# A hybrid encoder trunk: the two gated heads of a pair end together, and their farthest level is computed as keys times values, then queries

## The chip, the core and the metric

The kernel runs on one core of one Trainium2 chip. The metric is device microseconds of one execution. The engines that matter here are TensorE (PE: matmuls and transposes), VectorE (DVE), ScalarE (ACT: activations, copies out of PSUM, and DMA issues on its own queue), and SyncE (SP), whose queue loads most weights. Each engine works through its own instructions strictly in the order in which the program stands for it, and semaphores make it wait for the others.

## The reference, cut to what matters

Two layers work on 512 tokens of width 1024, in float32. Each is a half-step feed-forward block, a mixer, and a second half-step block. The mixer is where the change lies:

```python
proj = rmsnorm(x, mix_norm) @ w_in          # na_q, na_k, na_v, g_q, g_k, g_v, g_r, gate codes
na_o  = rmsnorm(merge_heads(neighbourhood_attention(na_q, na_k, na_v, na_rpb)), na_gain)   # 8 heads of 64
log_g = log_sigmoid(code @ w_gate + b_gate) / 16          # one for each direction
o_fwd = gla_chunked(qg, kg, vg, log_gf, True)             # 4 gated heads, keys 64 wide, values 128 wide
o_bwd = flip(gla_chunked(flip(qg), flip(kg), flip(vg), flip(log_gb), False))
gla_o = merge_heads(rmsnorm(o_fwd + o_bwd, gla_gain)) * silu(g_r)
x = x + concatenate([na_o, gla_o]) @ w_out
```

Gated linear attention is a sum over earlier (forward) and later (backward) tokens of `(q_t . decayed k_s) v_s`. The kernel computes it as a hierarchy of levels: a token pair whose distance first shows at block size h is handled at level h, where keys and queries carry the decay up to the border between two neighbouring blocks of h tokens. The farthest level, h = 256, joins the two halves of the sequence.

## The kernel before, in words

Activations lie transposed: 128 channels on partitions, 512 tokens along the free axis. A float32 product with a weight tile is made of three fp32r matmuls: `split` cuts an operand into a rounded high part (ACT) and the remainder (DVE), and `mm3` multiplies high by high, high by low, low by high. Products between activations use plain float32.

**Streams.** `mixer` runs four generators through `interleave`: `gla_all(0)` (gated heads 0 and 1), `na_all` (neighbourhood attention), `gla_all(1)` (gated heads 2 and 3), and `fillers`, the projections that remain, then the output projection. A stream yields either a key that must be in `got`, or a pair of planned times. In each round every stream that is ready takes its steps, then waiting transposes (`turns`) are made, then the filler gets about `SLOT` = 5.3 planned microseconds. This sets the program's order. For TensorE that order is kept (`pinned`). The other engines' instructions are put in an order of their own by the scheduler of the build, so the code doesn't tell it; the built program does.

**Fillers.** `PAIRS` is the order of the projection tiles. `v..` are neighbourhood values, `gv..` gated values, `gr..` the gates that pass through silu. A gated value tile is transposed (`turn`) before use. After the last tile, `op_part(c, 0, 4)` multiplies the neighbourhood half by `w_out` for the eight output tiles c; then come, for c below 4, heads 0 and 1 (`op_part(c, 4, 2)`), and behind the mixer, in the stage that the profile calls OP, heads 2 and 3 (`op_part(c, 6, 2)`) and all four gated heads for the c above.

**Gated heads.** `gla_levels(pr)` builds, for both heads of pair pr, the matrices `at` (levels up to 64), `am` (level 128) and `af` (level 256, four tiles of 128x512). `gla_out` sums values times these in PSUM, takes the root mean square over the head's 128 channels, scales, and multiplies by silu of the gate.

**The row of a root mean square.** `rsqrt_ms` is used for the neighbourhood row and for every gated head: the squares are split (`sqh` on ACT, `sql` on DVE), two matmuls with ones sum them into the bank `bank`, and `rsqrt_row` evaluates it:

```python
MM(ps, onr, h, start=True, stop=False)
MM(ps, onr, l, start=False, stop=True)
...
S.activation(r, ps, AF.Ln, bias=epsc, scale=1.0 / n)
S.activation(r, r, AF.Exp, scale=-0.5)
S.activation(t, ps, AF.Identity, bias=epsc, scale=1.0 / n)
```

In the profile these are `M_r<-M_tp` (Ln), `M_ms<-M_tp` (Identity) and `M_r<-M_r` (Exp), followed by three DVE operations.

**PSUM.** It has eight banks of 128x512: four named `mm`, two `sc`, and one each of `tp` and `o`. Every transpose goes through the one `tp` bank and has to wait until ACT has copied the one before out of it; `rsqrt_ms` uses `tp`, or `sc` for the second head of a pair.

**SBUF pools.** `TAGS` gives the number of 128x512 buffers for each tag; `g0` and `g1` hold everything of pair 0 and of pair 1.

Of the kernel before, what the change touches and what calls it, by code (L numbers as in the profile page):

```python
# [26 lines left out]
FAL = 1.4  # L27
HEAD = 9
MMB = 4
GOT = ('mm', 'mm')  # L30
WARM = 13
NAP = 4.0
SLOT = 5.3
# [10 lines left out]
         ('gk1', 'gq1'),  # L44
         ('q3', 'k3'),
         ('v2', 'v3'),
         ('gr0', 'gr1'),
         ('gv2', 'gv3'),
         ('gv0', 'gv1'),
         ('gr2', 'gr3'))  # L50
COLS = {"q": 0, "k": 512, "v": 1024, "gq": 1536, "gk": 1792, "gv": 2048, "gr": 2560}
TAGS = {'sl': 12, 'g0': 8, 'g1': 8, 'na': 6, 'ws': 5}
NPR = 12
NDF = 3
OPT = 2.56
# [5 lines left out]
def trunk_kernel(ctx, tc, xin, wgu, wdn, win, wcode, wgate, wout, vec, rpbt,  # L61
# [39 lines left out]
    def sl(name="s", dt=F32, tag="sl"):  # L101
        return sp.tile([P, T], dt, tag=tag, name=nm(name), bufs=TAGS[tag])
# [11 lines left out]
    def psum(tag):  # L114
        pool = {"mm": pm, "sc": ps2}.get(tag, ps1)
        return pool.tile([P, T], F32, tag=tag, name=nm(tag))
# [7 lines left out]
    def MM(*args, **kw):  # L124
        return pinned(PE.matmul(*args, **kw))  # L125

    def TR(*args):
        return pinned(PE.transpose(*args))  # L128
# [48 lines left out]
    def paired(mms):  # L177

        for ps, lhs, rhs, kw in mms:
            MM(ps, lhs, rhs, **kw)  # L180
# [396 lines left out]
    def seq_out(a):  # L577
        return a.rearrange("p (r u c) -> p u r c", r=8, u=8)

    def unit_in(a):  # L580
        return a.rearrange("p (u r c) -> p u r c", u=8, r=8)

    def mixer(l):
# [25 lines left out]
        gla = [{}, {}]  # L609

        def gla_gates(pr):
            g = gla[pr]
            for d in range(2):
                gs, pk = sl("gs", F32, f"g{pr}"), sl("pk", F32, f"g{pr}")
                pg = psum("sc" if pr == 0 else ("o", "tp")[d])
                cs = slice(d * 256 + pr * P, d * 256 + (pr + 1) * P)
                MM(pg, wgh[:, cs], cr, start=True, stop=False)
                MM(pg, wgl[:64, cs], cr[:64], start=False, stop=True)
                b = lvec(l, 5 + 2 * d + pr)
                ab, mn = sl("ab", F32, "ws"), sl("mn", F32, "ws")  # L620
                S.activation(ab, pg, AF.Abs, bias=b)
                V.tensor_scalar(mn, pg, b, 0.0, ALU.add, ALU.min)
                S.activation(ab, ab, AF.Exp, scale=-1.0)
                S.activation(ab, ab, AF.Ln, bias=1.0)
                V.tensor_tensor(gs, mn, ab, op=ALU.subtract)
                prev = gs
                for h in (2, 4, 8, 16, 32, 64, 128):
                    n = T // h
                    cur = pk[:, GOFF[h]:GOFF[h] + n]
                    pv = prev.rearrange("p (b two) -> p two b", two=2)  # L630
                    V.tensor_tensor(cur, pv[:, 0, :], pv[:, 1, :], op=ALU.add)
                    prev = cur
                S.activation(gs, gs, AF.Exp, scale=1.0 / 16.0)
                S.activation(pk[:, :508], pk[:, :508], AF.Exp, scale=1.0 / 16.0)
                g["t1", d], g["tp", d] = gs, pk
# [11 lines left out]

        def gla_levels(pr):
            g = gla[pr]
            gla_gates(pr)  # L650
            yield 1.8, 6.0
            yield ("gq", pr)
            qa, ka = got["gq", pr], got["gk", pr]
# [41 lines left out]
            for li, h in enumerate((1, 2, 4, 8, 16, 32, 64, 128)):  # L695
# [45 lines left out]
                elif h2 == 128:  # L741
                    pss = psum("sc"), psum("sc")
                    mms = []
                    for s in range(4):
                        t = s ^ 1
                        kk, qq = (KF, QF) if s < t else (KB, QB)
                        mms += [(pss[hh][:, s * P:(s + 1) * P], kk[rows[hh], s * P:(s + 1) * P],
                                 qq[rows[hh], t * P:(t + 1) * P], SS) for hh in (1, 0)]
                    paired(mms)
                    for hh in range(2):  # L750
                        g["m", hh] = sl("am", F32, f"g{pr}")
                        S.activation(g["m", hh], pss[hh], AF.Copy)
                    done = 1.0
                else:
                    for half in range(2):
                        pss = psum("sc"), psum("sc")
                        kk, qq = (KF, QF) if half == 0 else (KB, QB)
                        o = 256 * (1 - half)
                        paired([(pss[hh][:, j * 256:(j + 1) * 256],
                                 kk[rows[hh], (2 * half + j) * P:(2 * half + j + 1) * P], qq[rows[hh], o:o + 256], SS)  # L760
                                for j in range(2) for hh in (1, 0)])
                        for hh in range(2):
                            g["f", hh, half] = sl("af", F32, f"g{pr}")
                            S.activation(g["f", hh, half], pss[hh], AF.Copy)
                        yield 1.0, FAL

        def post_gv(h0):
            def post(i, o, r):
# [25 lines left out]
        def osplit(src, k, gain):  # L794
            ohl[k] = pair("oh", gain, src)

        def gla_out(hd, tag):
            g = gla[hd // 2]
            hh = hd % 2
            yield ("gs", hd)  # L800
            yield ("gv", hd)
            po = psum(tag)
            v = got["gv", hd]

            def vs(s):
                return v[:, s * P:(s + 1) * P]

            for t in range(4):
                dst = po[:, t * P:(t + 1) * P]
                half = 1 - t // 2  # L810
                fa = g["f", hh, half]
                s1 = t ^ 1
                MM(dst, vs(t), g["at"][hh][:, t * P:(t + 1) * P], start=True, stop=False)
                MM(dst, vs(s1), g["m", hh][:, s1 * P:(s1 + 1) * P], start=False, stop=False)
                for j in range(2):
                    o = j * 256 + (t % 2) * P
                    MM(dst, vs(2 * half + j), fa[:, o:o + P], start=False, stop=(j == 1))
            tag = GOTT[hd // 2]
            on, sq = sl("on", F32, tag), sl("sq", F32, tag)
            S.activation(sq, po, AF.Square)  # L820
            S.activation(on, po, AF.Copy, scale=0.125)
            got["po", hd] = True
            yield OUTT, 1.0
            r = rsqrt_ms(sq, 64 * P, False, tag, ("tp", "sc")[hh])
            V.tensor_tensor(on, on, r, op=ALU.mult)
            gp = got["gr", hd]
            V.tensor_tensor(unit_in(gp), seq_out(on), unit_in(gp), op=ALU.mult)
            osplit(gp, 4 + hd, lvec(l, 4))
            got["oh", hd] = True
            yield 0.9, 0.0  # L830


        def vmat_steps(src, done):
# [163 lines left out]
        def fillers():  # L997
# [13 lines left out]
            for c in range(KD):  # L1011
# [2 lines left out]
                V.tensor_tensor(o, pss[c], got["na"], op=ALU.mult)  # L1014
                V.tensor_tensor(xt[:, c, :], xt[:, c, :], o, op=ALU.add)
                yield OPT, 0.0
            for hd in (1, 3):
                yield ("po", hd)
            yield ("oh", 0)
            yield ("oh", 1)  # L1020
# [14 lines left out]

        def gla_all(pr):
            yield from gla_levels(pr)
            for hd in (2 * pr, 2 * pr + 1):
                yield from gla_out(hd, GOT[pr])

        raw, ws = st.pop("dpre", (None, None))
        b0 = dmat(win[l, 0], ("mm", "mm"), raw, ws)
# [177 lines left out]
```

## Time and profile before

| | |
|---|---|
| three timed runs | 1922.54, 1924.27, 1924.54 us (median 1924.27) |
| the profiled execution: its time, its span | 1924.05 us, 1922.3 us |
| TensorE busy | 1897.2 us, 99% of the span |
| VectorE, ScalarE busy | 1407.5 us (73%), 1034.9 us (54%) |
| granted TensorE clock, mean | 0.998 of full speed |

The time lies 1.75 us above the span. A busy TensorE includes the drain of the last matmul before an idle stretch, so start times tell more than busy times. `M_` marks the mixer of either layer, `F_` the feed-forward blocks, `OP_` what follows the mixer's four streams. Layer 1's mixer lies at about 357 to 611 us, layer 2's at about 1309 to 1560 us. Names of tiles are those of the code: `tp`, `sc`, `mm`, `o` are banks.

### The profile page before, as it was taken

What the parts mean: (1) busy time and instruction counts of PE and PEld (TensorE: products, weight loads), DVE (VectorE), ACT (ScalarE), POOL (GpSimd) and SP (SyncE); (2) the same over time, 40 slices, a digit from 0 to 9 for tenths busy, and PEclk for the clock granted to TensorE, in tenths of its full rate; (3) what the DMA queues carried; (4) which work ended last, traced back from release to release, by engine and by line L of the source; (5) the groups of instructions that cost most, each with busy time, mean ns of one, the idle gap of its engine ahead of it and who ended that gap; (6) DMA issues with size and microseconds to landing.
All of it is one profiled execution on the core that took longest, in us unless ns stands there. A gap on an engine that the chain in (4) does not pass through costs nothing.

```text
span 1922.3 us, 32197 instructions
## 1 busy us (share of the span) xinstructions
PE 1897.2 (99%) x12490; PEld 1674.1 (87%) x12490; DVE 1407.5 (73%) x2695; ACT 1034.9 (54%) x1978; POOL 17.3 (1%) x36
## 2 busy tenths in 40 slices
PE   9999999999999999999999999999999999999997
PEld 8889989877887898989889899997887878999896
DVE  7958768676648976958787596776765689678585
ACT  6535536475765553635555264455666655446264
POOL 0000000000000000000000000000000000000000
PEclk9999999999999999999999999999999999999999
DMA  5332223322113233322332332232221133323322
GB/s 179 107 106 100 95 103 127 113 78 78 61 48 101 94 107 108 110 100 93 102 101 91 109 110 101 98 121 96 89 89 56 39 115 110 110 88 111 110 78 77
DMA packets 58249, 187.78 MB, mean 98 GB/s; under 512 B 6640, under 2 KB 13296, under 8 KB 45808
## 3 DMA queue, kind: packets, MB, share of 16 engines
q1 hardware_dynamic: 30480, 133.12, 20.2%
q10 hardware_dynamic: 25056, 44.22, 7.0%
q0 software_dynamic: 2560, 8.39, 1.4%
q8 instruction: 98, 1.61, 0.3%
q14 instruction: 55, 0.45, 0.1%
HBM read 183.60 MB, written 2.10 MB: 97 GB/s over the span
## 4 chain that ended last, share of the span: by engine, by line
PE 91%; DVE 4%; ACT 3%; issue 1%; DMA 1%; ACTq 0%; DVEq 0%
PE F_mm L125 42%; PE F_sc L125 27%; PE M_mm L125 14%; PE M_sc L125 2%; PE F_tp L125 1%; PE F_o L125 1%; PE M_tp L128 1%; PE M_o L125 1%; PE OP_mm L125 1%; PE M_tp L125 1%; DVE M_on L1014 0%; DVE OP_wl L159 0%; PE I_o L125 0%; DMA OP_wraw<-in_wgu 0%; DVE M_a L268 0%
## 5 line engine op out<-in xcount | busy, mean ns | idle before, releaser
L125 PE MATMUL F_mm<-F_xc,F_wh 128*128 128x256 f32 x3584 | 638.3, 282 | 1.7 <-ACT F_o L310 1.2
L125 PEld LDWEIGHTS F_mm<-F_xc,F_wh 128*128 128x128 f32 x3584 | 553.8, 190 | 5.7 <-ACT F_o L310 1.5
L158 ACT ACTIVATE F_wh<-F_wraw 128x512 fp32r<-128x512 f32 (+1 forms) x472 | 289.0, 617 | 435.1 <-PE F_sc L125 240.5
L125 PE MATMUL F_mm<-F_xc,F_wl 128*128 128x256 f32 x1792 | 496.6, 282 | 0.0
L125 PE MATMUL F_sc<-F_hid,F_wh 128*128 128x512 f32 (+1 forms) x1432 | 438.8, 387 | 1.3 <-DVE xt L479 1.3
L159 DVE TENSOR_TENSOR F_wl<-F_wraw,F_wh 128x512 fp32r<-128x512 f32 (+1 forms) x472 | 313.4, 670 | 147.4 <-ACT F_wh L158 141.1
L125 PEld LDWEIGHTS F_mm<-F_xc,F_wl 128*128 128x128 f32 x1792 | 336.4, 190 | 0.0
L125 PEld LDWEIGHTS F_sc<-F_hid,F_wh 128*128 128x128 f32 x1432 | 265.7, 188 | 54.6 <-DVE xt L479 3.0
L125 PE MATMUL F_sc<-F_hid,F_wl 128*128 128x512 f32 (+1 forms) x716 | 276.7, 386 | 0.0
L158 ACT ACTIVATE F_wh<-F_ws 128x512 fp32r<-128x512 f32 x256 | 161.6, 632 | 165.1 <-PE F_mm L125 104.7
L159 DVE TENSOR_TENSOR F_wl<-F_ws,F_wh 128x512 fp32r<-128x512 f32 x256 | 174.9, 689 | 39.2 <-ACT F_wh L158 36.4
L125 PE MATMUL M_mm<-F_xd,M_wh 128*128 128x512 f32 x608 | 193.7, 399 | 0.0
L125 PEld LDWEIGHTS F_sc<-F_hid,F_wl 128*128 128x128 f32 x716 | 134.6, 188 | 26.5
L479 DVE SCALAR_TENSOR_TENSOR xt<-F_sc,xt 128x512 f32<-128x512 f32 x94 | 65.0, 691 | 96.8 <-PE F_sc L125 96.2
L125 PEld LDWEIGHTS M_mm<-F_xd,M_wh 128*128 128x128 f32 x608 | 112.4, 189 | 24.7 <-issue 1.9
L159 DVE TENSOR_TENSOR M_wl<-M_wraw,M_wh 128x512 fp32r<-128x512 f32 (+1 forms) x112 | 74.2, 669 | 62.3 <-ACT M_wh L158 44.0
L125 PE MATMUL M_mm<-F_xd,M_wl 128*128 128x512 f32 x304 | 119.5, 393 | 0.0
L158 ACT ACTIVATE M_wh<-M_wraw 128x512 fp32r<-128x512 f32 (+1 forms) x112 | 67.9, 616 | 67.8 <-PE M_mm L125 48.8
L125 PEld LDWEIGHTS M_mm<-F_xd,M_wl 128*128 128x128 f32 x304 | 57.4, 189 | 12.5
L125 PE MATMUL F_mm<-OP_xd,F_wh 128*128 128x512 f32 x224 | 67.4, 390 | 0.0
L159 DVE TENSOR_TENSOR F_hid<-F_o,F_hid 128x512 fp32r<-128x512 f32 x88 | 60.4, 689 | 1.3
L158 ACT ACTIVATE F_hid<-F_o 128x512 fp32r<-128x512 f32 x88 | 54.7, 625 | 5.2 <-DVE F_o L414 3.8
(298 smaller groups left out, 2645.7 us busy)
## 6 DMA issues: line engine op xcount, KB each, us to landing
F_wraw<-in_wgu SPq DMA_DIRECT2D x64, 1024.0 KB, 4.8
F_wraw<-in_wdn SPq DMA_DIRECT2D x32, 1024.0 KB, 4.9
M_wraw<-in_win ACTq DMA_DIRECT2D x88, 256.0 KB, 3.6
F_wraw<-in_wgu ACTq DMA_DIRECT2D x76, 256.0 KB, 3.7
F_wraw<-in_wdn SPq DMA_DIRECT2D x16, 768.0 KB, 4.2
M_pp<-in_rpbt POOLq DMA_DIRECT2D x32, 256.0 KB, 3.5
M_wraw<-in_wout SPq DMA_DIRECT2D x16, 256.0 KB, 2.7
xt<-in_xin SPq DMA_DIRECT2D x8, 256.0 KB, 5.2
```

Of the source, the lines that this page charges most:

```text
L125: return pinned(PE.matmul(*args, **kw))
L128: return pinned(PE.transpose(*args))
L158: S.activation(h, src, AF.Copy)
L159: V.tensor_tensor(l, src, h.bitcast(F32), op=ALU.subtract)
L479: V.scalar_tensor_tensor(xt[:, c, :], pss[j], 0.5, xt[:, c, :], ALU.mult, ALU.add)
```

## The change

For the farthest level, TensorE no longer forms the four score tiles `af`. The decayed keys are transposed (four 128x128 transposes into `tp`, one copy to `ks`), `gla_state` multiplies them with the values into a 64x128 state for each head and direction, which ACT copies into a zeroed tile `st`, and each head multiplies `st` with the decayed queries: one matmul for each quarter of the tokens in place of two.

`gla_heads` replaces `gla_out`. Both heads' sums are made one after the other, without waiting for the gates' silu; then both rows of root mean squares, then both products with the gates. `gv` tiles move ahead of `gr` tiles in `PAIRS`. The gates' codes of pair 1 use the bank `o` twice, with a pause between, in place of `o` and `tp`. The output projection's second part now waits for the sums of all four heads. Tag `g0` gets a ninth buffer.

```diff
-         ('gr0', 'gr1'),
-         ('gv2', 'gv3'),
-         ('gv0', 'gv1'),
+         ('gv0', 'gv1'),
+         ('gv2', 'gv3'),
+         ('gr0', 'gr1'),
          ('gr2', 'gr3'))
...
-TAGS = {'sl': 12, 'g0': 8, 'g1': 8, 'na': 6, 'ws': 5}
+TAGS = {'sl': 12, 'g0': 9, 'g1': 8, 'na': 6, 'ws': 5}
...
-                pg = psum("sc" if pr == 0 else ("o", "tp")[d])
+                if pr and d:
+                    yield 0.9, 3.0
+                pg = psum("o" if pr else "sc")
...
-                    for half in range(2):
-                        pss = psum("sc"), psum("sc")
-                        kk, qq = (KF, QF) if half == 0 else (KB, QB)
-                        o = 256 * (1 - half)
-                        paired([(pss[hh][:, j * 256:(j + 1) * 256],
-                                 kk[rows[hh], (2 * half + j) * P:(2 * half + j + 1) * P], qq[rows[hh], o:o + 256], SS)
-                                for j in range(2) for hh in (1, 0)])
-                        for hh in range(2):
-                            g["f", hh, half] = sl("af", F32, f"g{pr}")
-                            S.activation(g["f", hh, half], pss[hh], AF.Copy)
-                        yield 1.0, FAL
+                    pt = psum("tp")
+                    for i in range(4):
+                        TR(pt[:, i * P:(i + 1) * P], (KF if i < 2 else KB)[:, i * P:(i + 1) * P], idn)
+                    g["ks"], g["q"] = sl("ks", F32, f"g{pr}"), (QF, QB)
+                    S.activation(g["ks"], pt, AF.Copy)
+                    yield 0.5, FAL
+
+        def gla_state(pr):
+            g = gla[pr]
+            for hd in (2 * pr, 2 * pr + 1):
+                yield ("gv", hd)
+            ps = psum("sc")
+            rows = slice(0, 64), slice(64, P)
+            paired([(ps[rows[hh], half * P:(half + 1) * P],
+                     g["ks"][:, (2 * half + j) * P + hh * 64:(2 * half + j) * P + hh * 64 + 64],
+                     got["gv", 2 * pr + hh][:, (2 * half + j) * P:(2 * half + j + 1) * P],
+                     dict(start=j == 0, stop=j == 1))
+                    for half in range(2) for j in range(2) for hh in (1, 0)])
+            g["st"] = sl("st", F32, f"g{pr}")
+            V.memset(g["st"], 0.0)
+            for hh in range(2):
+                S.activation(g["st"][rows[hh], hh * H2:(hh + 1) * H2], ps[rows[hh], :H2], AF.Copy)
+            yield 0.6, FAL
...
-        def gla_out(hd, tag):
...
-                for j in range(2):
-                    o = j * 256 + (t % 2) * P
-                    MM(dst, vs(2 * half + j), fa[:, o:o + P], start=False, stop=(j == 1))
...
+        def gla_heads(pr):
+            for hh, hd in enumerate((2 * pr, 2 * pr + 1)):
+                yield ("gv", hd)
+                po = psum("mm")
...
+                    MM(dst, g["st"][:, hh * H2 + h * P:hh * H2 + (h + 1) * P], g["q"][h][:, t * P:(t + 1) * P],
+                       start=False, stop=True)
+                on, sq = sl("on", F32, tag), sl("sq", F32, tag)
+                S.activation(sq, po, AF.Square)
+                S.activation(on, po, AF.Copy, scale=0.125)
+                got["po", hd] = True
+                heads.append((hd, on, sq))
+                yield OUTT / 2, 0.0
+            yield 0.0, 1.0
+            for hh, (hd, on, sq) in enumerate(heads):
+                r = rsqrt_ms(sq, 64 * P, False, tag, ("tp", "sc")[hh])
+                V.tensor_tensor(on, on, r, op=ALU.mult)
+                yield 0.5, 0.0
+            for hd, on, sq in heads:
+                yield ("gs", hd)
+                gp = got["gr", hd]
+                V.tensor_tensor(unit_in(gp), seq_out(on), unit_in(gp), op=ALU.mult)
+                osplit(gp, 4 + hd, lvec(l, 4))
+                got["oh", hd] = True
...
-            for hd in (1, 3):
+            for hd in range(4):
                 yield ("po", hd)
```

How the instructions then stand. **First place**, TensorE, the end of layer 1's fillers, where the rows of root mean squares are summed. Before, head 0's row (5945) is followed by the products of head 1 (`mm_5966`), then comes the neighbourhood row (5987), then the products of head 2 (`mm_6003`); both rows use bank `tp`:

```order
L125 MATMUL M_tp_5945<-M_sqh_5946,onr 128x512
L125 MATMUL M_tp_5945<-M_sql_5947,onr 128x512
L125 MATMUL M_mm_5966<-M_at_4866,M_gv_5920 128x128
L125 MATMUL M_mm_5966<-M_am_4961,M_gv_5920 128x128
L125 MATMUL M_mm_5966<-M_af_5202,M_gv_5920 128x128 x2
...
L125 MATMUL M_tp_5987<-M_sqh_5988,onr 128x512
L125 MATMUL M_tp_5987<-M_sql_5989,onr 128x512
L125 MATMUL M_mm_6003<-M_at_5636,M_gv_5728 128x128
```

In the changed program the neighbourhood row, head 2's row (again in bank `tp`) and head 3's row (in `sc`) stand next to each other, and the output projection follows:

```order
L124 MATMUL M_tp_6034<-M_sqh_6035,onr 128x512
L124 MATMUL M_tp_6034<-M_sql_6036,onr 128x512
L124 MATMUL M_tp_6050<-M_sqh_6051,onr 128x512
L124 MATMUL M_tp_6050<-M_sql_6052,onr 128x512
L124 MATMUL M_sc_6067<-M_sqh_6068,onr 128x512
L124 MATMUL M_sc_6067<-M_sql_6069,onr 128x512
L124 MATMUL M_mm_6092<-M_oh_4705,M_wh_6095 128x512 x2
```

What moved: the heads' products that stood between the rows of one bank now lie ahead of all three rows.

**Second place**, ScalarE at the same point of the changed program, from the neighbourhood row's Ln to the split of head 3's squares (`M_sqh_6068<-M_sq_6008`), which TensorE's fifth row above reads. `M_gr` is the silu of a gate:

```order
L260 ACT_TABLE_LOAD
L260 ACTIVATE M_r_6042<-M_tp_6034,vecs 128x512
L263 ACTIVATE M_ms_6041<-M_tp_6034,vecs 128x512
L261 ACT_TABLE_LOAD
L261 ACTIVATE M_r_6042<-M_r_6042 128x512
L804 ACT_TABLE_LOAD
L804 ACTIVATE M_gr_6029<-M_gr_6029 128x512
L242 ACT_TABLE_LOAD
L260 ACTIVATE M_r_6058<-M_tp_6050,vecs 128x512
L263 ACTIVATE M_ms_6057<-M_tp_6050,vecs 128x512
L261 ACTIVATE M_r_6058<-M_r_6058 128x512
L157 ACTIVATE M_sqh_6068<-M_sq_6008 128x512
```

In the program before, the same loads stand at head 0's row; behind the last of them come a head's two copies out of PSUM, and the squares of that head are split between the next row's Ln and Exp:

```order
L787 ACT_TABLE_LOAD
L787 ACTIVATE M_gr_5940<-M_gr_5940 128x512
L243 ACT_TABLE_LOAD
L820 ACTIVATE M_sq_5984<-M_mm_5966 128x512
L821 ACTIVATE M_on_5983<-M_mm_5966 128x512
L261 ACTIVATE M_r_5995<-M_tp_5987,vecs 128x512
L264 ACTIVATE M_ms_5994<-M_tp_5987,vecs 128x512
L158 ACTIVATE M_sqh_6091<-M_sq_5984 128x512
L262 ACTIVATE M_r_5995<-M_r_5995 128x512
```

What moved: the split of the last head's squares now stands behind the whole row of the head before it on ScalarE.

**Third place**, TensorE behind the products of heads 0 and 1 (layer 1). Before, the transposes of `pp` (neighbourhood probabilities) and `vt` (a gated value tile) are apart:

```order
L128 MATMUL M_tp_5765<-con,M_pp_5438 128x128 x4
L125 MATMUL M_sc_5772<-M_ga_4890 128x256
L125 MATMUL M_sc_5771<-M_ga_4890 128x256
L125 MATMUL M_sc_5772<-M_ga_4890 128x256
L125 MATMUL M_sc_5771<-M_ga_4890 128x256
L128 MATMUL M_tp_5781<-con,M_vt_5668 128x128 x4
L125 MATMUL M_mm_5758<-F_xd_3673,M_wh_5750 128x512 x2
```

In the changed program three tiles go through the `tp` bank in a row; a gate's tile (`mm_5769`) follows, and a little later the rows of heads 0 and 1:

```order
L127 MATMUL M_tp_5810<-con,M_pp_5425 128x128 x4
L127 MATMUL M_tp_5816<-con,M_ga_4890 128x128 x4
L127 MATMUL M_tp_5823<-con,M_vt_5666 128x128 x4
L124 MATMUL M_mm_5769<-F_xd_3673,M_wh_5761 128x512 x2
...
L124 MATMUL M_tp_5873<-M_sqh_5874,onr 128x512
L124 MATMUL M_tp_5873<-M_sql_5875,onr 128x512
L124 MATMUL M_sc_5890<-M_sqh_5891,onr 128x512
L124 MATMUL M_sc_5890<-M_sql_5892,onr 128x512
```

On ScalarE the two copies of head 1's sums (`sq` and `on`) come just ahead of the first row here, which splits head 0's squares; `M_gr_5848` is the silu of the gate above:

```order
L157 ACTIVATE M_sqh_5874<-M_sq_5790 128x512
L970 ACTIVATE M_pp_5425<-M_tp_5810 128x512
L762 ACTIVATE M_ks_5821<-M_tp_5816 128x512
L794 ACTIVATE M_gv_5828<-M_tp_5823 128x512
L157 ACTIVATE M_wh_6095<-M_wraw_6093 128x512
L157 ACTIVATE M_wh_6117<-M_wraw_6115 128x512
L804 ACTIVATE M_gr_5848<-M_gr_5848 128x512
L242 ACT_TABLE_LOAD
L260 ACTIVATE M_r_5881<-M_tp_5873,vecs 128x512
L263 ACTIVATE M_ms_5880<-M_tp_5873,vecs 128x512
L261 ACTIVATE M_r_5881<-M_r_5881 128x512
L157 ACTIVATE M_sqh_5891<-M_sq_5807 128x512
```

What moved: score matmuls left the place between two transposes, the transposes of the keys took it, and the split of head 1's squares stands behind head 0's row on ScalarE.

## Rows read from the trace of the kernel before

**Rows 1.** The page's first part: busy time, share, instructions

```profile
PE 1897.2 (99%) x12490; PEld 1674.1 (87%) x12490; DVE 1407.5 (73%) x2695; ACT 1034.9 (54%) x1978; POOL 17.3 (1%) x36
```

**Rows 2.** Waits of TensorE: what waited, for what; us in total, times, longest

```profile
PE M_tp L128 <- DVE M_mn L622: 3.2, 2, 1.6
PE OP_mm L125 <- DVE OP_wl L159: 2.3, 2, 1.1
PE OP_mm L125 <- ACT OP_wh L158: 1.8, 3, 0.8
PE M_sc L125 <- ACT M_am L752: 1.3, 1, 1.3
PE OP_mm L125 <- DVE xt L1063: 0.6, 2, 0.3
```

**Rows 3.** Timeline of TensorE: start us, duration us, then the instructions

```profile
461.46 1.38 PE L125 MATMUL M_sc<-M_ga,M_gkq 64*64 64x64 f32 x32 [1.32 <-ACT M_am L752]
462.76 0.76 PE L125 MATMUL M_mm<-F_xd,M_wh 128*128 128x512 f32 x2
...
467.20 0.63 PE L125 MATMUL M_mm<-F_xd,M_wh 128*128 128x512 f32 x2
...
467.89 0.63 PE L125 MATMUL M_mm<-F_xd,M_wh 128*128 128x512 f32 x2
...
471.76 0.66 PE L125 MATMUL M_o<-M_pp,M_vm 128*64 128x128 f32 x8
...
472.78 0.72 PE L125 MATMUL M_sc<-M_ga,M_kt 64*64 64x64 f32 x32
```

**Rows 4.** The same view, layer 1's gated heads and rows

```profile
528.98 0.60 PE L128 MATMUL M_tp<-con,M_pp 128*128 128x128 f32 x4
529.51 1.14 PE L125 MATMUL M_sc<-M_ga 64*128 64x256 f32 x8
530.58 0.66 PE L128 MATMUL M_tp<-con,M_vt 128*128 128x128 f32 x4
530.99 0.71 PE L125 MATMUL M_mm<-F_xd,M_wh 128*128 128x512 f32 x2
...
545.13 0.61 PE L125 MATMUL M_mm<-M_af,M_gv 128*128 128x128 f32 x4
545.58 0.39 PE L125 MATMUL M_mm<-M_at,M_gv 128*128 128x128 f32 x2
...
552.84 0.39 PE L125 MATMUL M_tp<-M_sqh,onr 128*128 128x512 f32 x1
```

**Rows 5.** Timeline of ScalarE in the same stretch

```profile
529.62 0.60 ACT L949 ACTIVATE M_pp<-M_tp 128x512 f32<-128x512 f32 x1 [1.35 <-PE M_tp L128]
...
553.46 1.28 ACT L261 ACT_TABLE_LOAD   x1
554.75 0.69 ACT L261 ACTIVATE M_r<-M_tp,vecs 128x512 f32<-128x512 f32 x1
...
561.22 0.60 ACT L820 ACTIVATE M_sq<-M_mm 128x512 f32<-128x512 f32 x1
...
562.19 0.69 ACT L261 ACTIVATE M_r<-M_tp,vecs 128x512 f32<-128x512 f32 x1
562.76 0.70 ACT L264 ACTIVATE M_ms<-M_tp,vecs 128x512 f32<-128x512 f32 x1
563.33 0.65 ACT L158 ACTIVATE M_sqh<-M_sq 128x512 fp32r<-128x512 f32 x1
563.85 0.65 ACT L262 ACTIVATE M_r<-M_r 128x512 f32<-128x512 f32 x1
```

**Rows 6.** Timeline of VectorE: a split's remainder

```profile
552.79 0.69 DVE L159 TENSOR_TENSOR M_wl<-M_wraw,M_wh 128x512 fp32r<-128x512 f32 x1 [1.51 <-PE M_mm L125]
```

**Rows 7.** Windows: us, busy PE, PEld, DVE, ACT, POOL; clock; DMA; GB/s

```profile
395.00:400.00 5.00, 3.95 (x20) 3.33 (x21) 5.00 (x16) 3.00 (x7) 0.00 (x0) 1.00 0.22 64
...
464.00:466.00 2.00, 2.00 (x6) 1.51 (x6) 1.93 (x9) 0.85 (x3) 0.00 (x0) 0.50 0.00 0
```

More of the change, by code (lines that the diff above doesn't have):

```diff
@@ L29 @@
 MMB = 4
-GOT = ('mm', 'mm')
 WARM = 13
@@ L649, in gla_levels @@
             g = gla[pr]
-            gla_gates(pr)
+            yield from gla_gates(pr)
             yield 1.8, 6.0
@@ L795, in osplit @@
             ohl[k] = pair("oh", gain, src)
-        def gla_out(hd, tag):
[L798 to L814, printed above, removed]
-                for j in range(2):
-                    o = j * 256 + (t % 2) * P
-                    MM(dst, vs(2 * half + j), fa[:, o:o + P], start=False, stop=(j == 1))
[L818 to L830, printed above, removed]
@@ new lines, in gla_heads, with vs @@
+        def gla_heads(pr):
+            g = gla[pr]
+            tag = GOTT[pr]
+            heads = []
+            for hh, hd in enumerate((2 * pr, 2 * pr + 1)):
+                yield ("gv", hd)
+                po = psum("mm")
+                v = got["gv", hd]
+                def vs(s):
+                    return v[:, s * P:(s + 1) * P]
+                for t in range(4):
+                    h = 1 - t // 2
+                    dst = po[:, t * P:(t + 1) * P]
+                    s1 = t ^ 1
+                    MM(dst, vs(t), g["at"][hh][:, t * P:(t + 1) * P], start=True, stop=False)
+                    MM(dst, vs(s1), g["m", hh][:, s1 * P:(s1 + 1) * P], start=False, stop=False)
+                    MM(dst, g["st"][:, hh * H2 + h * P:hh * H2 + (h + 1) * P], g["q"][h][:, t * P:(t + 1) * P],
[17 more added lines that the diff above has]
+                got["oh", hd] = True
@@ L1037, in gla_all @@
             yield from gla_levels(pr)
-            for hd in (2 * pr, 2 * pr + 1):
-                yield from gla_out(hd, GOT[pr])
+            yield from gla_state(pr)
+            yield from gla_heads(pr)
         raw, ws = st.pop("dpre", (None, None))
```

## The prediction

> **What bounds the kernel now.** I read the page's busy times first: TensorE is busy 99% of the span, ScalarE 54%, VectorE 73% [rows 1]. So the time is TensorE's work plus its few waits; an engine off this path matters only where TensorE has to wait for it. Then I read TensorE's waits [rows 2]: the largest group is 3.2 us, twice 1.6, a transpose that waits for a gate's VectorE work in the `tp` bank; the OP stage has 2.3 + 1.8 + 0.6 = 4.7 us. Since TensorE's order is fixed, what the change does is read off in two columns: products removed, and new waits made by the new neighbours in its order. For the second I went through TensorE's new order row by row and asked of each row that must wait for a copy or a split where that stands in ScalarE's or VectorE's order. The timelines [rows 3 to 6] give the durations. I quote start-to-start distances, because durations overlap in a pipelined engine.
>
> **Part 1, work removed.** For each pair of heads:
> - The score matmuls of level 256: one half takes 529.51 to 530.58, 1.07 us [rows 4]; two halves, -2.14.
> - In a head's sum, the two `af` matmuls of a quarter take 545.13 to 545.58, 0.45 [rows 4]. One matmul remains, of the same form, so half: 0.225 x 4 quarters x 2 heads = -1.80.
> - New: four transposes, 530.58 to 530.99, +0.41 [rows 4]; the state's eight matmuls, not in the trace. The rows count two passes for a float32 product, so the nearest are the two groups `M_o`, 16 passes together on a tile of the same size: 471.76 to 472.78, +1.02 [rows 3]. Bounds 0.5 (as if it were one group) to 1.1.
>
> Together -2.5 a pair, -5.0 a layer (bounds -4.9 to -6.0). The copies of four `af` tiles become one of `ks` and two small ones; ScalarE has 46% idle time, so this is worth nothing by itself, nor is a memset on VectorE.
>
> **Part 2, waits removed.** The second gate now uses bank `o`, behind a pause, so the transpose no longer waits for VectorE in `tp`: -1.6 a layer [rows 2]. The ninth buffer costs space only. In OP, VectorE is behind (its `wl` splits and residual adds are what TensorE waits for). If TensorE arrives there some us later, as the next part says, VectorE and ScalarE have caught up. Idle there is 2.35 a layer [rows 2], start-to-start somewhat more, since a matmul behind a wait runs slower at first; I take -2.0, bounds 0 to -3.4. Gains in all: 8.6 a layer.
>
> **Part 3, waits added.** Four places in each layer, in program order.
> - A, pair 0: the keys' transposes stand right ahead of a `pp` tile's. Now the bank's copy decides: transposes at 528.98, copy from 529.62, 0.60 long [rows 4, 5], so the next tile may start 1.24 after the first, in place of 0.41: +0.8.
> - B, behind the products of heads 0 and 1: three tiles in a row through `tp`, and ScalarE must first do `sq` and `on` of head 1 (561.22 to 562.19, 0.97) and a split (0.52, as 563.33 to 563.85) [rows 5], before the copy of `pp`. Count from the first transpose, T. The last product drains until T + 0.2; sq and on until 1.2; split until 1.7; copy until 2.3; second tile at 2.3, its copy 2.9 to 3.5; third tile at 3.5, next matmul at 3.9. Without waits 3 x 0.41 = 1.2. So +2.7 (bounds 2.2, if head 1's copies start as early as the transposes, to 3.2).
> - C, the rows of heads 0 and 1: the split of head 1's squares stands behind head 0's Ln, Identity and Exp. A silu ends at about the row's start; then the table load, 1.29 (553.46 to 554.75), Ln 0.57, Identity 0.57, Exp 0.52 (a row as long as the split's), split 0.65, VectorE's remainder 0.69 [rows 5, 6], and the last matmul 0.23: 0.1 + 4.5 = 4.6 behind the row's start, against 4 x 0.23 = 0.9 (a 128x512 pass is 0.69 / 3 = 0.23, 467.20 to 467.89 [rows 3]): +3.7. If the silu is earlier, the load is hidden and it is 2.4; if the load waits for the row, 4.2.
> - E, the neighbourhood row, head 2's and head 3's, one behind the other: all that ScalarE did before between 553.46 and 561.22 behind such a row (four table loads, Ln, Identity, Exp, a silu) stands ahead of head 2's Ln. The row began at 552.84 [rows 4]; call that U. Head 2's row follows when Ln and Identity have left the bank, at U + 3.2, but its Ln starts only at U + 8.4. Then Ln 0.57, Identity 0.57, Exp 0.52, split 0.65: U + 10.7; remainder 0.69, matmul 0.23: U + 11.6. Without waits 6 x 0.23 = 1.4. So +10.2. Before, 16 products of another head lay between the rows, and the waits show none for such a row [rows 2]. Behind E stands the output projection, which therefore starts that much later; nothing on TensorE can pass it.
>
> A to E sum to +17.4 a layer. The loads that stand ahead of an activation without a wait may run early; only the first of E's four could, -0.6 (553.46 is 0.6 behind U). The other three lie between activations that need each other's engine time, so they cost their length.
>
> **Part 4, the clock.** [...] What follows there lost 2.3 us: the group at 461.46 lasted 1.38 where the same form took 0.72 at 472.78, and the twelve passes from 462.76 to 467.20 took 4.44 in place of 12 x 0.23 = 2.76 [rows 3]. [...]
>
> **Sum.** A layer: -5.0 - 1.6 - 2.0 + 17.4 + 2.3 = +11.1; two layers +22.2. The order at these places is the same in layer 2. The profiled execution took 1924.05, 0.2 below the median of the runs (1924.27): 1924.05 + 22.2 = 1946.3. What layer 1 lost at 461, 1.3 + 2.3 = 3.6 us with its wait, isn't touched by the change and may or may not come again: 0 to -3.6.
>
> **Rivals.**
> 1. *Faster.* The split of a row's squares isn't held up as the order says: ScalarE has done it before TensorE arrives, C and E vanish and with them the clock's loss. Then a layer is A + B - 8.6 = 3.5 - 8.6 = -5.1: 1914. It is decided at C + E + clock = 5.1 a layer. For it: no row in the waits of before has TensorE waiting for such a split [rows 2]. Against it: the split stands behind Ln and Exp of the row ahead in the built program. 0.10. Where C + E + clock come to 3.2 to 7.1 the change is within 0.2% (about what a measurement of this kernel can tell from none): 0.05.
> 2. *The clock stays at full.* 1946.3 - 4.6 = 1942; with the OP stage's waits wholly gone (another 1.4 a layer) 1939. The window 395 to 400 speaks for it. 0.22.
> 3. *The clock falls behind B and C too.* Two times 2.3 more a layer: 1946.3 + 9.2 = 1955.5. The loss at 461 behind only 1.32 us speaks for it, the window at 395 against. 0.20. [...]
> 4. *A switch of tables costs more than its load.* In the trace the next activation starts 1.29 behind the load's start [rows 5], so nothing is added. If each of the five loads in C and E cost about twice that, it would be 5 x 1.3 x 2 = 13 more: 1959. 0.04. [...]
>
> **How the numbers follow.** My forecast, all four waits with one clock loss a layer: 0.39; rivals as above: 0.10, 0.05 (no change), 0.22, 0.20, 0.04. The range runs from 2 with the whole OP relief and without layer 1's loss (1939 - 3.6, about 1936) to a little above 4 (1960); outside lie rival 1 and the no-change case. Faster 0.10, same 0.05, slower 0.85.
>
> **What would show it.** Right: TensorE waits for `M_sqh` in two places of each layer (about 10 and 4 us), for `M_pp`, `M_ks` copies in one (about 2.7); a window near 0.5 to 0.8 of the clock behind the last row; no wait for `M_mn`; a head's sum of twelve products in 2.7 us. Wrong: head 3's split done before the neighbourhood row, or a wait of the new state for `M_ks`, which I put at none as whole filler tiles lie between; or score and sum savings that differ from 5.0.

## The result, and the profile after

| | before | changed |
|---|---|---|
| median of the runs | 1923.95 us (1922.54 to 1924.54, 4 runs) | 1948.94 us (1948.11 to 1949.52, 4 runs) |
| ratio | 1 | 1.0131, 95% interval 1.0113 to 1.0148 |
| TensorE busy, span | 1897.2 of 1922.3 us | 1897.1 of 1947.7 us |

The change costs 25.0 us; 22.2 were forecast. The first part of the changed kernel's page, to be read beside [rows 1]:

```profile
PE 1897.1 (97%) x12442; PEld 1672.8 (86%) x12442; DVE 1411.8 (72%) x2699; ACT 1029.3 (53%) x1970; POOL 17.4 (1%) x36
```

TensorE has 48 instruction records fewer and is as long busy: what the new form saved is offset by matmuls that ran slowly, as shown below. The time came as idle time. Its waits, as in [rows 2] (us in total, times, longest):

```profile
PE M_sc L124 <- ACT M_sqh L157: 20.7, 4, 6.8
PE M_tp L124 <- ACT M_ms L263: 5.2, 2, 2.6
PE M_tp L127 <- ACT M_pp L970: 3.5, 2, 1.7
PE M_tp L127 <- ACT M_ks L762: 2.8, 4, 0.7
PE M_o L124 <- ACT M_vm L902: 2.4, 4, 0.8
PE M_sc L124 <- ACT M_am L754: 1.3, 1, 1.3
```

The wait for `M_mn` and all waits of OP are gone; 32 us of new ones stand in the first four rows, the same in both layers. TensorE's timeline shows layer 1's stretch of [rows 3] first, then the four places that the prediction called A, B, C and E:

```profile
460.74 1.37 PE L124 MATMUL M_sc<-M_ga,M_gkq 64*64 64x64 f32 x32 [1.34 <-ACT M_am L754]
462.04 0.73 PE L124 MATMUL M_mm<-F_xd,M_wh 128*128 128x512 f32 x2
...
464.92 0.62 PE L124 MATMUL M_mm<-F_xd,M_wh 128*128 128x512 f32 x2
...
467.71 0.60 PE L127 MATMUL M_tp<-con,M_ga 128*128 128x128 f32 x4
469.00 0.66 PE L127 MATMUL M_tp<-con,M_pp 128*128 128x128 f32 x4 [0.69 <-ACT M_ks L762]
...
518.34 1.09 PE L124 MATMUL M_sc<-M_gv,M_ks 128*64 128x128 f32 x16
519.37 0.66 PE L127 MATMUL M_tp<-con,M_pp 128*128 128x128 f32 x4
...
533.39 0.60 PE L127 MATMUL M_tp<-con,M_pp 128*128 128x128 f32 x4
535.73 0.66 PE L127 MATMUL M_tp<-con,M_ga 128*128 128x128 f32 x4 [1.74 <-ACT M_pp L970]
537.07 0.66 PE L127 MATMUL M_tp<-con,M_vt 128*128 128x128 f32 x4 [0.69 <-ACT M_ks L762]
537.48 0.71 PE L124 MATMUL M_mm<-F_xd,M_wh 128*128 128x512 f32 x2
...
543.05 0.39 PE L124 MATMUL M_tp<-M_sqh,onr 128*128 128x512 f32 x1
...
547.27 0.80 PE L124 MATMUL M_sc<-M_sqh,onr 128*128 128x512 f32 x1 [3.59 <-ACT M_sqh L157]
...
548.80 1.12 PE L124 MATMUL M_o<-M_pp,M_vm 128*64 128x128 f32 x8
...
550.56 1.92 PE L124 MATMUL M_sc<-M_gv,M_ks 128*64 128x128 f32 x16
552.41 1.02 PE L124 MATMUL M_mm<-F_xd,M_wh 128*128 128x512 f32 x2
...
567.74 0.39 PE L124 MATMUL M_tp<-M_sqh,onr 128*128 128x512 f32 x1
...
570.97 0.50 PE L124 MATMUL M_tp<-M_sqh,onr 128*128 128x512 f32 x1 [2.60 <-ACT M_ms L263]
...
578.47 0.79 PE L124 MATMUL M_sc<-M_sqh,onr 128*128 128x512 f32 x1 [6.77 <-ACT M_sqh L157]
...
579.87 0.63 PE L124 MATMUL M_mm<-M_oh,M_wh 128*128 128x512 f32 x1
```

Read it by start times: A 467.71 to 469.00 (1.29), B 533.39 to 537.48 (4.09), C 543.05 to 548.80 (5.75), E 567.74 to 579.87 (12.13). Layer 2 has the same four places at 1430.13, 1495.84, 1505.50 and 1530.26, each as long to within 0.01 us. The same eight `M_gv,M_ks` products take 1.03 us at 518.34 and 1.85 at 550.56: the second stand behind C. The clock in windows behind B and over C and E (columns as in [rows 7]) says why:

```profile
538.00:543.00 5.00, 5.00 (x23) 4.12 (x22) 1.36 (x3) 1.66 (x4) 0.00 (x0) 1.00 0.00 0
543.00:548.00 5.00, 1.41 (x4) 0.48 (x3) 1.80 (x4) 4.19 (x6) 0.00 (x0) 0.82 0.34 105
548.00:553.00 5.00, 4.99 (x35) 4.07 (x35) 4.86 (x9) 2.95 (x6) 0.00 (x0) 0.50 0.02 3
...
568.00:573.00 5.00, 1.11 (x4) 0.30 (x2) 1.69 (x4) 4.92 (x7) 0.00 (x0) 1.00 0.32 107
573.00:578.00 5.00, 0.00 (x0) 0.00 (x0) 2.04 (x4) 4.96 (x7) 0.00 (x0) 0.56 0.00 0
578.00:583.00 5.00, 4.51 (x10) 3.23 (x11) 4.86 (x8) 2.92 (x5) 0.00 (x0) 0.50 0.00 0
```

TensorE works at 0.50 of its clock behind C and E, and at 1.00 behind B. And ScalarE in E, from the last work ahead of the row to head 3's split:

```profile
567.03 1.31 ACT L157 ACTIVATE M_wh<-M_wraw 128x512 fp32r<-128x512 f32 x2 [1.44 <-PE M_mm L124]
568.36 1.28 ACT L260 ACT_TABLE_LOAD   x1
569.65 0.69 ACT L260 ACTIVATE M_r<-M_tp,vecs 128x512 f32<-128x512 f32 x1
...
576.12 0.69 ACT L260 ACTIVATE M_r<-M_tp,vecs 128x512 f32<-128x512 f32 x1
...
577.79 0.63 ACT L157 ACTIVATE M_sqh<-M_sq 128x512 fp32r<-128x512 f32 x1
```

ScalarE isn't idle between 567.03 and 578.4. Head 2's Ln starts at U + 8.4 with U = 567.74, as forecast; the split starts at U + 10.05, where the prediction's terms give U + 10.06.

### The profile page after: what moved, and what is told of

Its sections match the earlier page's. It is cut to its first block, busy times and chain, and to the rows that moved or that the text cites. A ratio compares the mean times of both kernels' runs of the same rounds, so it can differ in the third digit from the quotient of the medians.

```text
span 1947.7 us, 32103 instructions
## 1 busy us (share of the span) xinstructions
PE 1897.1 (97%) x12442; PEld 1672.8 (86%) x12442; DVE 1411.8 (72%) x2699; ACT 1029.3 (53%) x1970; POOL 17.4 (1%) x36
## 4 chain that ended last, share of the span: by engine, by line
PE 94%; ACT 3%; DVE 2%; issue 0%; ACTq 0%; DVEq 0%
PE F_mm L124 42%; PE F_sc L124 27%; PE M_mm L124 17%; PE M_sc L124 2%; PE F_tp L124 1%; PE OP_mm L124 1%; PE F_o L124 1%; PE M_tp L127 1%; PE M_o L124 1%; PE M_tp L124 1%; PE I_o L124 0%; DVE M_wl L158 0%; ACTq L345 0%; ACT L242 0%; ACT M_wh L157 0%
```

## The experiments

Times are medians, ratios are to runs of the kernel before on the same chip at the same time (its medians: 1921.73 us for the first four runs, 1923.08 for the next four, 1922.96 for the last four). Where a run is set against the changed kernel, the difference of the two ratios counts; 0.1% is 1.9 us, and as each ratio is known to 0.1 to 0.2% either way, such a difference is known to about 4 us. Where that is too coarse, start times of the two traces are compared. Fences of waits give us in total, times and longest, as above.

**1. Early splits.**

```diff
                 S.activation(on, po, AF.Copy, scale=0.125)
+                hl = sl("sqh", F32R, tag), sl("sql", F32R, tag)
+                split(sq, *hl)
...
-                r = rsqrt_ms(sq, 64 * P, False, tag, ("tp", "sc")[hh])
+                ps = psum(BANK[hh])
+                MM(ps, onr, hl[0], start=True, stop=False)
+                MM(ps, onr, hl[1], start=False, stop=True)
+                r = rsqrt_row(ps, 64 * P, *(sl(k, F32, "ws") for k in ("ms", "r", "a")), act=True)
```

`BANK` is `('tp', 'sc')`, the banks of the change.

Expected: 

> The changed kernel, with each gated head's squares split (rounded part and remainder) right behind the head's products, ahead of the rows, in place of between the rows. TensorE's order stays. Theory (the waits are made by ScalarE's order: the second head's split stands behind the first head's Ln, Exp and table loads): the 3.6 us and 6.8 us waits for the split in each layer vanish, with the clock's loss behind them; the wait of head 2's row for the bank stays or grows to 3 to 5 us. About 12 us a layer back: 1920 to 1927. Rival (the waits come from the table loads and the silu standing there, wherever the split is): TensorE waits as long for another row, 1940 or more.

Measured 1921.39 us, ratio 0.9996 (0.9987 to 1.0006), in the expected range: 26 us below the changed kernel by the ratios, level with before. C is gone, and E's waits in layer 1 are three short ones:

```profile
561.44 0.50 PE L125 MATMUL M_tp<-M_sqh,onr 128*128 128x512 f32 x1 [1.01 <-ACT M_sqh L158]
562.77 0.49 PE L125 MATMUL M_tp<-M_sql,onr 128*128 128x512 f32 x1 [0.83 <-DVE M_sql L159]
564.82 0.50 PE L125 MATMUL M_tp<-M_sqh,onr 128*128 128x512 f32 x1 [1.55 <-ACT M_ms L264]
```

The first two are the neighbourhood row's own split, which now came behind two weight splits on ScalarE. The edit moved one thing more: in E one table load stood on ScalarE in place of four. Run 9 takes these apart.

**2. The new level alone** (with the ninth buffer), put into the kernel before, head by head.

```diff
...
-                    MM(dst, vs(2 * half + j), fa[:, o:o + P], start=False, stop=(j == 1))
+                MM(dst, g["st"][:, hh * H2 + h * P:hh * H2 + (h + 1) * P], g["q"][h][:, t * P:(t + 1) * P],
+                   start=False, stop=True)
...
             yield from gla_levels(pr)
+            yield from gla_state(pr)
```

Expected: 

> The kernel before, with level 256 alone changed to keys times values, then queries (and the ninth buffer that it needs); the order of the projection tiles, the gates and the head-by-head order are as before. Theory: the new form saves 5.0 us of TensorE work a layer and brings only small waits through the tp bank (0 to 3 us a layer): 1914 to 1920. Rival: the form itself costs as much as it saves, through copies and transposes: 1922 to 1930.

Measured 1932.28, ratio 1.0051 (1.0036 to 1.0066): a miss on both sides. One new wait stands in each layer, on TensorE's timeline of layer 1:

```profile
583.95 0.40 PE L125 MATMUL M_mm<-M_oh,M_wl 128*128 128x512 f32 x1
592.13 1.58 PE L125 MATMUL M_mm<-M_oh,M_wh 128*128 128x512 f32 x2 [7.78 <-ACT M_oh L161]
...
598.46 0.40 PE L125 MATMUL M_mm<-M_oh,M_wl 128*128 128x512 f32 x1
```

The state needs both heads' values, which come last in the old order of tiles; the heads end late, and the output projection reaches their products before ScalarE has split them, which itself waits for VectorE (3.3 and 1.9 us, for the splits that start at 588.76 and 591.35). From the first two rows TensorE stood 8.0 us, and the 14 passes to the last one took 6.3 in place of 3.2. Taken off in both layers that leaves about 1910, 11 below before: compatible with a saving of 10 by the form, but only by subtraction, in which 4.2 us of new waits in the `tp` bank (for `M_ks` and `M_pp`) stand against the 4.7 of OP, which are gone here too.

**3. The gates alone**, in the kernel before.

```diff
...
+                if pr and d:
+                    yield 0.9, 3.0
-                pg = psum("sc" if pr == 0 else ("o", "tp")[d])
+                pg = psum("o" if pr else "sc")
```

Expected: 

> The kernel before, with the gates of pair 1 alone changed: bank o twice with a pause, in place of o and tp. Theory: the 1.6 us wait of a transpose in each layer goes and nothing takes its place: 1920.5 to 1921.5. Rival: the second gate's matmul or the next transpose waits instead: 1923 to 1925.

Measured 1920.87, ratio 0.9992 (0.9983 to 1.0002). The wait for `M_mn` is gone, and TensorE's waits for `M_vm` rose from 1.3 to 2.4 us in both layers together, as they did in the changed kernel. That fits a gain of 2 us, but the time alone can't be told from no gain.

**4. Matmuls of zeros in the waits.**

```diff
+                n = ((0, 15), (11, 29))[pr][hh]
+                if n:
+                    pz = psum("sc")
+                    for _ in range(n):
+                        MM(pz[:, :P], zero, zero, start=True, stop=True)
                 r = rsqrt_ms(sq, 64 * P, False, tag, ("tp", "sc")[hh])
```

Expected: 

> The changed kernel, with matmuls of zeros, which nobody reads, put into the waits: 15 (about 3.3 us) ahead of head 1's row, 11 (2.4 us) ahead of head 2's and 29 (6.4 us) ahead of head 3's, each a little shorter than the wait. Theory (behind a wait of 4 us and more TensorE runs at the lower clock, and that costs): the clock stays at 1.00 there, the rows end when they did, and what follows isn't slowed: 4 to 6 us a layer less, 1938 to 1942. Rival (the slow rows are there because of something else, or the matmuls push the rows back): 1948 to 1956.

Measured 1940.37, ratio 1.0095 (1.0080 to 1.0110): 110 useless matmuls make the changed kernel 7 us faster by the ratios. The windows over C, and those over E (565 to 585), are at full clock, 1.00, and the state is back to 1.04 us of busy time:

```profile
543.00:548.00 5.00, 4.45 (x34) 3.85 (x33) 1.80 (x4) 3.95 (x6) 0.00 (x0) 1.00 0.35 105
548.00:553.00 5.00, 5.00 (x45) 4.12 (x46) 4.86 (x8) 3.27 (x6) 0.00 (x0) 1.00 0.02 3
```

```profile
543.28 3.51 PE L124 MATMUL M_sc<-zero 128*128 128x128 f32 x30
...
549.19 1.04 PE L124 MATMUL M_sc<-M_gv,M_ks 128*64 128x128 f32 x16
```

From the first pass of C to the end of the slow passes behind E, layer 1 took 40.66 us in the changed kernel (543.05 to 583.71) and takes 36.33 here (542.81 to 579.14); layer 2 took 40.73 and takes 36.34. So the clock cost 4.3 to 4.4 us a layer: C's and E's losses, not one. The profiled execution is 7.4 us faster and not 8.7 because the clock fell elsewhere: behind B of layer 2, whose waits were 1.75 and 0.69 us as in the changed kernel, it was 0.50 (1496 to 1498), and the stretch from B to C took 1.6 us longer.

**5. The new level and the order of tiles**, heads one at a time: run 2 with `gv` ahead of `gr` in `PAIRS`.

Expected: 

> The kernel before with two parts of the change: level 256 as keys times values, then queries, and the gated values' tiles ahead of the gates'. Heads one at a time and gates as before. In the run with the state alone, one wait of 7.8 us a layer appeared, for the heads' split products at the output projection's second part. Theory (the state needs both heads' values, which come last there, so the heads end late): with the values earlier the heads end earlier, that wait goes, and the 5.0 us a layer show: 1910 to 1917. Rival (the wait is made by the head-by-head order itself): 7 us a layer stay, 1928 to 1934.

Measured 1929.08, ratio 1.0031 (1.0019 to 1.0043). That is the rival's time, but not by the rival's way: the wait for `M_oh` went, so its cause was named rightly. Still the 5 us a layer didn't show: the rows of the heads now wait themselves.

```profile
PE M_sc L125 <- DVE M_sql L159: 3.0, 2, 1.5
...
PE M_tp L125 <- DVE M_sql L159: 2.6, 2, 1.3
```

These are 2.8 us a layer. Most of what else is missing is the `tp` bank's waits (5.2 in all, for `M_ks` and `M_pp`) and slow matmuls behind both kinds of wait: in layer 1 nine passes from 532.70 took 3.73 us in place of 2.07, and a head's twelve products from 573.57 took 4.22, at a granted clock of 0.78 from 575 to 580, where they take 2.68 at full clock. Sums that wait for a split come in the head-by-head order too, once the tiles' order is changed with the level (run 2, with the old order of tiles, has none); my theory that the heads' old order spares them falls. The order of tiles alone was not run.

**6. The keys' transposes in a bank of sc.** `pt = psum("tp")` becomes `pt = psum("sc")` in `gla_levels`; all else as changed.

Expected: 

> The changed kernel, with the keys' transposes in a bank of sc in place of tp. Theory (waits A and B are the one tp bank's): the 0.7 us wait of pair 0 goes and the place with three tiles keeps only the wait for the copy of pp: 2 us a layer, 1944 to 1946. Rival (a tile in sc waits for the copies of scores instead, or ScalarE's order is what counts): 1948 to 1951.

Measured 1943.32, ratio 1.0103 (1.0087 to 1.0118): 5.4 us less than the changed kernel by the ratios, where 3 to 5 were expected. The four waits for `M_ks` are gone, and B keeps one wait of 1.3. In layer 1 A is 0.9 us shorter and B 1.3; another 1.3 are shorter slow stretches behind C and E in this execution. A and that part of B were the one bank's.

**7 and 8. All rows in sc; gated values' transposes in sc too.** Run 7 is run 1 with `BANK = ('sc', 'sc')`, the edit of run 6, and on ScalarE the weight splits of the output projection's later tiles ordered behind the neighbourhood split. Run 8 adds `pt = psum("sc")` in `post_gv`.

Expected of 7: 

> The changed kernel with early splits (as in the run before), both heads' rows in the two banks of sc, the keys' transposes in sc, and the split of the neighbourhood squares kept ahead of two splits of weights on ScalarE. Theory: the waits left with early splits (bank 1.5, neighbourhood split 1.9, keys' tiles 1.4 us a layer, and slower starts behind them) go: 1908 to 1914. Rival (rows in sc wait for the copies of the state, or the neighbourhood row waits for its sum anyway): 1917 to 1922.

Expected of 8: 

> As e7_splits_banks, with the gated values' transposes in sc too. Theory (the third tile in a row still waits for the copy of pp in tp, about 0.8 us a layer): 1.5 to 2 us less than that run, 1906 to 1912. Rival (these transposes wait for the copies of scores in sc): 1 to 4 us more than that run.

Measured 1923.33, ratio 1.0002 (0.9993 to 1.0010), and 1935.67, ratio 1.0065 (1.0053 to 1.0078); both misses. In run 7 the three rows no longer wait, but two other waits came:

```profile
PE M_mm L125 <- ACT M_wh L159: 5.6, 2, 2.8
...
PE M_sc L125 <- ACT M_ms L269: 2.1, 2, 1.1
```

The forced order brought three table loads back into ScalarE's stretch behind the row (at 558.49, 561.07 and 563.02 in layer 1), and the weights' splits among and behind them freed the raw weights' buffers late; ScalarE then waited for the next load itself:

```profile
572.80 0.42 ACT L159 ACTIVATE M_wh<-M_wraw 128x256 fp32r<-128x256 f32 x1 [2.60 <-DMA M_wraw<-in_wout]
```

The link from the splits to the late load is argued from the two buffers of `wraw`, not shown by a run. The second wait is the state's, for a bank that a row holds. Run 8's transposes wait for copies of scores:

```profile
PE M_sc L128 <- ACT M_at L747: 6.4, 2, 3.2
```

**9. The silu first, splits late.** In `rsqrt_row`, the neighbourhood row's Ln is ordered behind the last gate's silu on ScalarE, which leaves one load in E.

```diff
-        S.activation(r, ps, AF.Ln, bias=epsc, scale=1.0 / n)
+        ln = S.activation(r, ps, AF.Ln, bias=epsc, scale=1.0 / n)
+        if n == 512:
+            tc.add_manual_dep(ln.ins, st["silu"].ins.name, mybir.DependencyInfo(
+                mybir.DependencyClass.NoSync, mybir.DependencyReason.DATA), reason="behind silu")
...
-                        S.activation(got["gr", hd], got["gr", hd], AF.Silu)
+                        st["silu"] = S.activation(got["gr", hd], got["gr", hd], AF.Silu)
```

Expected: 

> The changed kernel, with ScalarE's Ln of the neighbourhood row kept behind the silu of the last gate, so that one table load stands in E in place of four; the splits stay late. Theory (E's wait is the sum of what stands on ScalarE ahead of head 3's split, loads at their own length): three loads go, E is 3.9 us shorter in each layer and the waits for head 3's split fall from 6.8 to 2 to 3 us, while C keeps its 3.6: 1938 to 1942. Rival (loads are hidden, or the split's late place alone decides): 1946 to 1950. By the other rival (a switch costs twice its load): 1931 to 1934.

Measured 1942.70, ratio 1.0097 (1.0082 to 1.0113): 6.5 us below the changed kernel by the ratios, where 7 to 11 were expected.

```profile
PE M_sc L124 <- ACT M_sqh L157: 11.9, 4, 3.6
PE M_tp L124 <- ACT M_ms L266: 7.8, 2, 3.9
```

Three loads of 1.28 went from ScalarE, but the silu now waits for VectorE's product, and only then Ln and Identity free the bank: that wait grew from 2.6 to 3.9 while the split's fell from 6.8 to 2.4. E now lasts 9.05 us (569.33 to 578.38), so the loads make 3.1 of its 12.1; the larger part of what run 1 gave back, in C and E together, is the splits' place. Run 7 agrees: three loads stand behind the row again, the splits are early, and the rows don't wait. No load was seen to cost more than its own length: behind the one load left in E (1.28 us) the next activation came 1.29 after the load's start (571.25 to 572.54).

**10 to 12. Towards a better kernel.** Run 10 is run 1 with the keys' transposes in sc. Run 11 has both rows of every pair in sc. Run 12 has heads 0 and 1 in `tp` and `sc`, heads 2 and 3 in the two banks of sc:

```diff
+BANK = (('tp', 'sc'), ('sc', 'sc'))
...
-                    pt = psum("tp")
+                    pt = psum("sc")
                     for i in range(4):
                         TR(pt[:, i * P:(i + 1) * P], (KF if i < 2 else KB)[:, i * P:(i + 1) * P], idn)
...
+                ps = psum(BANK[pr][hh])
```

Expected of 10: 

> The changed kernel with early splits and the keys' transposes in sc; rows in tp and sc as in the change. Theory: the gains add, 2 us a layer below the run with early splits alone: 1916 to 1919 beside 1921 to 1923 for the kernel before. Rival (something else then waits, as in e7): 1921 to 1924.

Expected of 11: 

> As e10, with both rows of every pair in the two banks of sc, and ScalarE's order left to the build. Theory: the wait of head 2's row for the bank (1.5 us a layer) goes, and a wait of the state for a row's bank (1.1 us, as in e7) comes: within 2 us of e10. Rival (the weights' splits come late again, as in e7): 1921 or more.

Expected of 12: 

> As e10, with rows in tp and sc for heads 0 and 1, and in the two banks of sc for heads 2 and 3. Theory: the wait for the bank goes and none comes: 1912 to 1916. Rival (a later wait takes its place): as e10.

Measured 1917.51, ratio 0.9968 (0.9955 to 0.9980); 1916.95, ratio 0.9968 (0.9956 to 0.9981); and 1913.90, ratio 0.9951 (0.9939 to 0.9964). All three went as the theory said, and run 12 beats both kernels: 9.1 us below before by the medians. Its page and its longest waits:

```profile
PE 1885.8 (99%) x12442; PEld 1664.5 (87%) x12442; DVE 1408.5 (74%) x2699; ACT 1022.3 (53%) x1964; POOL 17.3 (1%) x36
```

```profile
PE M_o L125 <- ACT M_vm L908: 2.3, 4, 0.7
PE M_tp L125 <- ACT M_sqh L158: 2.0, 2, 1.0
PE M_tp L125 <- DVE M_sql L159: 1.7, 2, 0.8
```

TensorE is busy 11.4 us less than before [rows 1]. Some 1.7 of it is the slow stretch of layer 1 [rows 3], which this profile doesn't have (from that group to the end of its twelve passes 4.06 in place of 5.74); 9.7 remain, 4.9 a layer: that is near the saving of the new form, forecast at 5.0.

## Why the prediction was right

The direction, the mechanism and each place were right; several terms were mis-sized, and they partly offset. That 22.2 lies so near 25.0 owes something to luck: the relief of OP, which was larger than forecast, and a slow stretch of layer 1 that didn't come again hide much of what C and the clock cost more. Layer 2, which had no disturbance of its own, gives the cleanest sum (us a layer; the places are as long in both layers, and the start times are layer 1's):

| term | forecast | measured | from |
|---|---|---|---|
| work removed | -5.0 | about -5 | state 1.03 against 1.02; a head's sum 2.68 (528.03 to 530.71), before 3.57 (544.69 to 548.26) |
| gate's wait | -1.6 | -1.6 | no `M_mn` row |
| OP | -2.0 | -3.4 | no OP row; by pairing the same matmuls there in both traces |
| A | +0.8 | +0.9 | 1.29 - 0.42 |
| B | +2.7 | +2.9 | 4.09 - 3 x 0.41 |
| C | +3.7 | +4.8 | 5.75 - 0.92 |
| E | +10.2 | +10.7 | 12.13 - 1.4 |
| clock behind C and E | +2.3 | +3.9 | 2.0 and 1.9, below |
| waits for `M_vm` | 0 | +0.5 | waits, 2.4 against 1.3 in all |
| sum | +11.1 | +13.7 | the layer took 13.6 more |

The layer's 13.6 is the shift of the first matmul behind the mixer: 1585.55 against 1560.12 us in layer 2, 25.4 in all, of which 11.8 were there at the same matmul of layer 1 (623.01 against 611.19). Layer 1's wait at 461 came again (1.34 us), but not the slow clock behind it: the same twelve passes took 2.88 us (462.04 to 464.92) in place of 4.44, at a granted clock of 1.00. That is 1.6 of the 1.8 us by which layer 1 moved less than layer 2.

**Part 1** holds: the state's products cost what the nearest row said. **Part 2**: OP's waits all went, the far bound of that term; I had kept some back for no reason that the rows gave. **Part 3**: A, B and E to within 0.5 us. C was taken with a silu that ends at the row's start; it ended 0.5 behind it (543.6 against 543.05), and the rest is slower matmuls. In the signs, head 3's split was given a wait of about 10 us; it was 6.8, as 2.6 us of E's standstill are the bank's. (E's times U + 3.2 and U + 10.7 give two standstills of 2.6 and 6.9; 2.60 and 6.77 were measured.) The gates' edit moved the waits for `M_vm`, which I had not priced; run 3 has them without the rest of the change.

**Part 4** is the step that failed, in its count: the forecast had "one clock loss a layer", +2.3, for E alone. No run shows that term as it was counted; in its place each layer of the changed kernel lost 2.0 us behind C and 1.9 behind E. C lost too, so rival 3 was half right, B lost nothing (clock 1.00 at 538 to 543). The loss behind C is 0.74 in the 16 passes of `M_o`, 0.82 in the state and 0.4 in the next products; behind E, 9 passes from 579.87 took 3.84 in place of 2.07, and 0.1 more. Run 4 measures the clock's price apart from the waits, with the rows inside C and E: 4.3 to 4.4 a layer. The size of one loss was misread too: of the 2.3 that stand for layer 1's loss at 461, 0.6 are the group at 461.46, during which the clock was 1.00 (461.46 to 462.76), and which took the same 1.30 us at 1.00 in the changed kernel (460.74 to 462.04). Why it is slower than the group at 472.78, which has other operands, no run shows; the passes behind it lost 1.7.

**The rivals.** Rival 1 (the splits are made in time) is what run 1 builds. It gives back 26 us, of the 32 at which C, E and the clock were priced for both layers, so the condition was the right one and the built order had failed it. Rival 2 falls with the windows at 0.50 and with run 4. Rival 4 falls: loads lasted 1.28 us, as before, and in C and E the next activation came 1.29 to 1.30 behind each load's start (568.36 to 569.65, 574.82 to 576.12).

What the time didn't show: the new level removes the work that was forecast (the heads' sums above, run 12's busy time), and every order of the heads tried here gave some of it back in waits for splits, banks or products. The smallest such waits, in run 12, leave 9 of the 13 us that the removed work and the gate's wait are worth; the three groups above hold much of the rest. The old level in run 12's order was not run, so what the level alone is worth in the time is not shown.

## What to carry to other kernels

When work is moved away from between two steps that share a bank or an in-order engine, ask what that work was covering: here a head's 16 products and part of the output projection lay ahead of the next row and hid ScalarE's work on the one before, and with rows side by side TensorE saw it. The wait is read off by counting, in the built order of the helping engine, everything ahead of the one instruction that TensorE needs; moving that instruction ahead gave back 26 us here, though what then came behind it could wait in its turn (runs 1 and 7). Price a long wait with the slow matmuls behind it, and at each place where there is one (here 2.0 us behind C's wait of 3.59 and 1.9 behind E's of 6.77); for waits of 1 to 2 us, allow for both outcomes (at 461 the twelve passes behind a wait of 1.32 took 4.44 us before, and 2.88 behind 1.34 in the changed kernel).

## What the runs showed of the hardware

The length of a wait alone doesn't say whether TensorE's clock falls. It was 0.50 behind the 3.59 us of C and the 6.77 of E, in both layers, and 1.00 in the window around E's first wait of 2.60. Two shorter waits had both outcomes: at 461 the clock was 0.50 from 463.3 on in the kernel before, behind 1.32 us [rows 3, 7], and again in run 9, behind 1.33, but 1.00 in the changed kernel, behind 1.34; behind B (1.74 and 0.69 us with a tile between) it stayed at 1.00 in both layers of the changed kernel and was 0.50 in layer 2 of run 4. What decides there, no run shows. In run 4, where products of zeros that nobody reads filled the waits, the clock was 1.00 in every window from 543 to 553 and from 565 to 585; in the changed kernel it was 0.82 and then 0.50 over the first stretch, and 0.56 and 0.50 from 573 to 583.
